# Hybrid decoder layer on one core: memory keys and values computed first, kept in DRAM, and x loaded from GpSimd's queue

## The chip, the cores and the metric

The kernel runs on one core of a Trainium2 chip. A core has five engines that run beside each other: TensorE (PE; its weight loads are shown as PEld), VectorE (DVE), ScalarE (ACT), GpSimd (POOL) and SyncE (SP), which here issues the DMAs. The metric is the device time of one execution in microseconds (us); lower is better. Before the change the median of 3 runs is 2018.0 us (2016.56 to 2018.23).

## What is computed

The reference is one layer of a decoder for a prompt of 1024 tokens and 8 single sample tokens, 1032 rows of width 1024 in all, in float32. Cut to what matters here:

```python
z = x @ w_in                                   # all branches and gates from one projection
xr, yr, q, k, v, xq, g = split(z)
a_out = rg_lru(conv4(xr)) * gelu(yr)           # branch A: a recurrence over the tokens
s_out = sliding_window_attention(q, k, v)      # branch B
mkv = mem_prompt @ w_mem_kv                    # 256 memory tokens -> keys mk, values mv (outputs too)
c_out = mem_attn(xq, mk, mv)                   # branch C: 4 heads of width 256
merged = sum(sigmoid(g_n + b_n) * (branch_n @ w_branch_n))
h = LN(alpha*x + merged @ w_out)
h = LN(alpha*h + SwiGLU(h))
```

The sample tokens use cached keys and values instead of `mk` and `mv`; their window buffers, moved on by one row, are outputs as well.

## The kernel before

Every float32 product is made of three faster ones. `split` (L69) makes a rounded high part on ScalarE and the low part, the difference, on VectorE; `mm3` (L100) then does high x high, high x low and low x high. So each operand of TensorE needs one ScalarE and one VectorE instruction first, and these are listed under L71 and L72 whatever they serve.

The input projection (`project`, L256) goes over 30 units of 256 output columns (`UNITS`, L37). Each is done by a scheme of seven products of quarter matrices (Strassen's, in Winograd's form) instead of eight, so it needs seven combinations of quarters of x. `combos` (L157) makes them, for each half p of the columns of the quarters: four loads (`x_quarter`, L149: 512 features by 258 tokens, 516 KB, issued on SP), four sums or differences, and seven splits into the tiles `th` and `tl` of the pool `tp`, where they stay until the projection ends. The x quarters and the combinations lie in a ring of nine tiles named `z`, which later holds the units' results (`za`, `zb`). The unit's weights come in four loads (`ur`, via `half_raw`, L80: a ring of six raw tiles of 512 columns); `fast_quarter` (L190) makes seven operands `u_0` to `u_6` of them; `fast_product` (L204, lines 212 to 214) does the matmuls into `ub`, `uc` and `ud`. Side jobs, the recurrence (`lru`, L633) and the memory attention of the sample tokens (`dec_mem`, L709), are stepped on by `pump` after every product.

After the projection comes `mem_attention` (L433). `load_mem` (L331) loads and splits the memory tokens. `mem_kv` (L341) computes for one head its two key tiles (`mk`, 24 matmuls each, weights from `wmk`) and its values (`mv`, 48 matmuls, weights from `wmv`), stores them as outputs through a single buffer `kvraw`, and splits them again for use. Each of the four calls stands between the steps of attention: `mem_queries` and `mem_scores` (L386), `mem_values` (L411), and `fill`, which puts in products of branch A's projection (`branch`, L568; `bra`), whose activations `load_branch` (L116) loads as `baL`. Their tiles (`slots0`) lie where `tp` lay. Windowed attention, `out_proj` and `ffn` follow and aren't touched.

The order in which instructions stand on an engine isn't that of the source: a scheduler sorts each engine's list by its own estimates when the kernel is built, within the dependencies. An engine then goes through its list in that order, waits included. `tc.issue_after(x)` asks the scheduler to place what is issued within it after x. A pool's ring of `bufs` tiles makes an instruction that writes a tile wait for the readers of the tile that it reuses.

Of the kernel before, what the change touches and what calls it, by code (L numbers as in the profile page):

```python
# [10 lines left out]
F32 = mybir.dt.float32  # L11
F32R = mybir.dt.float32r
AF = mybir.ActivationFunctionType
ALU = mybir.AluOpType
# [19 lines left out]
HT = T // 2  # L34
QN = T // 4
QS = 272
UNITS = (  # L37
# [16 lines left out]
class Builder:  # L54
# [94 lines left out]
    def x_quarter(self, kh, th, p):  # L149

        t = self.zt(f"x{kh}{th}{p}")
        t0 = HT * th + QN * p
        self.x_loaded = self.nc.sync.dma_start(t.rearrange("p (k n) -> p k n", k=4),
                                               self.io["xT"][:, 4 * kh:4 * kh + 4, t0:t0 + QN]).ins
        return t

    def combos(self, p, quarter):  # L157

        nc = self.nc
        b11, b21, b12, b22 = quarter(0, 0, p), quarter(1, 0, p), quarter(0, 1, p), quarter(1, 1, p)  # L160
        out = []

        def keep(src, i):
            hi, lo = (self.tp.tile([P, 4, QS], F32R, tag="t", name=f"t{e}{i}_{p}", bufs=28) for e in "hl")
            self.split(hi[:, :, :QN], lo[:, :, :QN], src.rearrange("p (k n) -> p k n", k=4))
            out.append((hi, lo))

        keep(b11, 0)
        t1 = self.zt(f"t1_{p}")
        nc.vector.tensor_sub(t1, b11, b12)  # L170
        keep(t1, 1)
        t2 = self.zt(f"t2_{p}")
        nc.vector.scalar_tensor_tensor(t2, t1, -1.0, b22, op0=ALU.mult, op1=ALU.subtract)
        keep(t2, 2)
        keep(b21, 3)
        t3 = self.zt(f"t3_{p}")
        nc.vector.tensor_sub(t3, b22, b12)
        keep(t3, 4)
        keep(b22, 5)
        t4 = self.zt(f"t4_{p}")  # L180
        nc.vector.scalar_tensor_tensor(t4, t2, -1.0, b21, op0=ALU.mult, op1=ALU.subtract)
        keep(t4, 6)
        return out

# [70 lines left out]

    def project(self):  # L256

        nc, io, tc = self.nc, self.io, self.tc
# [6 lines left out]
        n = len(UNITS)  # L265
# [42 lines left out]
    def v_rows(self, zs):  # L308

        nc, io = self.nc, self.io  # L310
        for blk in range(9):
# [7 lines left out]
            if blk == 7:  # L319
                vraw = self.sm.tile([P, 256], F32, tag="kvraw", name="pwv", bufs=1)  # L320
                nc.scalar.copy(vraw, ps)
                nc.sync.dma_start(io["o_pwv"], vraw)
# [7 lines left out]

    def load_mem(self):  # L331
        nc, io = self.nc, self.io
        self.memx = []
        for k in range(KT):
            hi, lo = (self.ph.tile([P, NM], F32R, tag="mem", name=f"mem{e}{k}", bufs=16) for e in "hl")
            if k % 2 == 0:
                raw = self.half_raw(io["memT"][:, k * NM:(k + 2) * NM], 2 * NM, f"mem{k}")
            self.split(hi, lo, raw[:, (k % 2) * NM:(k % 2 + 1) * NM])
            self.memx.append((hi, lo))

    def mem_kv(self, h):  # L341

        nc, io = self.nc, self.io
        mk, mv = [], []
        for m in (2 * h, 2 * h + 1):
            w = self.weights(io["wmk"][m], D, f"wmk{m}")
            ps = self.bank("mm", f"mk{m}")[:, :NM]
            self.mm3(ps, [(w[k], self.memx[k]) for k in range(KT)])
            raw = self.sm.tile([P, 256], F32, tag="kvraw", name=f"mkr{m}", bufs=1)
            nc.scalar.copy(raw, ps)  # L350
            nc.sync.dma_start(io["o_pmk"][:, m, :], raw)
            hi, lo = (self.ph.tile([P, NM], F32R, tag="mk", name=f"mk{e}{m}", bufs=6) for e in "hl")
            self.split(hi, lo, raw)
            mk.append((hi, lo))
        pv = [self.bank("mm", f"mv{h}_{tt}")[:, :256] for tt in range(2)]
        for j in range(4):
            raw = self.half_raw(io["wmv"][2 * h + j // 2][:, (j % 2) * 512:(j % 2 + 1) * 512], 512, f"wmv{h}_{j}r")
            wh, wl = self.half_pair(f"wmv{h}_{j}")
            self.last_split = self.split(wh, wl, raw)
            for tt in range(2):  # L360
                for i in range(2):
                    xh, xl = (a[:, tt * P:(tt + 1) * P] for a in self.memx[2 * j + i])
                    vh, vl = (a[:, i * 256:(i + 1) * 256] for a in (wh, wl))
                    nc.tensor.matmul(pv[tt], xh, vh, start=j + i == 0, stop=False)
                    nc.tensor.matmul(pv[tt], xh, vl, start=False, stop=False)
                    self.last_mm = nc.tensor.matmul(pv[tt], xl, vh, start=False, stop=j + i == 4).ins
        for tt, ps in enumerate(pv):
            raw = self.sm.tile([P, 256], F32, tag="kvraw", name=f"mvr{h}_{tt}", bufs=1)
            nc.scalar.copy(raw, ps)
            nc.sync.dma_start(io["o_pmv"][:, tt, h * 256:(h + 1) * 256], raw)  # L370
            hi, lo = (self.ph.tile([P, 256], F32R, tag="mv", name=f"mv{e}{h}_{tt}", bufs=8) for e in "hl")
            self.split(hi, lo, raw)
            mv.append((hi, lo))
        return mk, mv

# [257 lines left out]
    def lru(self, m, xr, yr):  # L633
# [3 lines left out]
        stt = nc.vector.scalar_tensor_tensor  # L637
        wr = self.z.tile([P, 256], F32, tag="wlr", name=f"wlr{m}", bufs=1)
# [12 lines left out]
        nc.gpsimd.tensor_copy(self.scvo[:, m, 2, :], xr[:, TP:T])  # L651
        wgh, wgl = (self.z.tile([P, 256], F32R, tag=f"wg{e}", name=f"wg{e}{m}", bufs=1) for e in "hl")
        self.split(wgh, wgl, wr)
        a, ti = self.zt(f"tr{m}"), self.zt(f"ti{m}")
        for c, (t0, n) in enumerate(THIRDS):
            xch, xcl = (self.z.tile([P, n], F32R, tag=f"xc{e}", name=f"xc{e}{m}_{c}", bufs=1) for e in "hl")
            self.split(xch, xcl, xc[:, t0:t0 + n])
# [110 lines left out]
    def dec_win_scores(self):  # L768
# [7 lines left out]
        for name, cache, row in (("o_swk", "cwk", krow), ("o_swv", "cwv", self.vd)):  # L776
            nc.sync.dma_start(io[name][:, 0:P - 1, :], io[cache][:, 1:P, :])
            nc.sync.dma_start(io[name][:, P - 1, :], row)
# [281 lines left out]
    def build(self):  # L1060
# [3 lines left out]
        shapes = {"c": [P, KT, T], "s": [P, KT, T], "a": [P, KT, T], "g": [P, 24, T], "xq": [P, KT, 2, TP],  # L1064
                  "q": [P, KT, 2, TP], "k": [P, 2, 2, TP], "v": [P, 8, 512]}
        self.scr = {b: self.dram.tile(n, F32, name=f"scr_{b}") for b, n in shapes.items()}
# [3 lines left out]
        self.ctx.enter_context(pool("edge", "right")).tile([P, 8], F32, name="edge")  # L1070
        with pool("tp", "right") as self.tp, pool("w1") as self.w1, pool("z") as self.z, pool("dp1") as self.dp:
            self.project()
        self.act, self.merged = {}, [[None] * 3 for _ in range(KT)]
# [26 lines left out]
class Finish:  # L1100
# [42 lines left out]
_INS = {  # L1143
    "xT": (P, KT, T), "memT": (P, KT * NM), "wmk": (KT, P, D), "wmv": (8, P, D), "win": (60, P, D),
    "wbr": (24, P, D), "wout": (KT, P, D), "wgu": (2 * NF, P, D), "wdn": (KT, P, NF * P), "wlru": (KT, P, 256),
# [10 lines left out]
def _pack(i):  # L1156
# [15 lines left out]
    x = np.concatenate([f["x_prompt"].reshape(TP, D), f["x_sample"].reshape(NB, D)], axis=0)  # L1172
    o["xT"] = x.T.reshape(KT, P, T).transpose(1, 0, 2)
    o["memT"] = f["mem_prompt"].reshape(NM, D).T.reshape(KT, P, NM).transpose(1, 0, 2).reshape(P, KT * NM)
    wkv = f["w_mem_kv"][0]
# [67 lines left out]
```

## Time and profile before

| | |
|---|---|
| median of 3 runs | 2018.0 us |
| profiled execution | 2021.07 us, of which the span of the trace is 2018.5 |
| granted clock of TensorE, mean | 0.993 |
| VectorE, ScalarE busy | 59%, 44% of the span |
| DMA queues | 235.42 MB, mean 117 GB/s; SP's queue alone 233.17 MB |
| instructions | 35388 |

The profile comes from one execution. A window row shows how long each engine was busy in a stretch. A timeline row has the start, the duration, the engine, the line of the kernel, the operation and its tiles (result <- sources); in brackets stands how long the engine was idle before it and what released it. A wait row sums such idle time: us in total, times, the longest. `L71 ACT ... th` is the high part of a combination of x, `L72 DVE ... tl` its low part.

### The profile page before, as it was taken

Reading aid. Unit: us, or ns where it says so; the run is one execution under the profiler, and the core shown is the slowest. Engines: PE = TensorE matmul, PEld = TensorE weight load, DVE = VectorE, ACT = ScalarE, POOL = GpSimd, SP = SyncE. Lnnn points to the kernel's source line nnn. Section 1 sums busy time; section 2 is a strip of 40 time slices with the busy share of each in tenths; the row PEclk is TensorE's granted clock in tenths of the full one; section 3 lists DMA queues with packets and bytes.
Section 4 is the critical chain, followed back from the end, with each engine's and each line's share of the span. In section 5 each row is a group of like instructions: output and inputs, shape, how many; then the busy total and the mean of one; then the engine's idle time right before and its main releaser. Section 6 shows DMA issues by size and latency. Waiting matters only on the chain.

```text
span 2018.5 us, 35388 instructions
## 1 busy us (share of the span) xinstructions
PE 1960.8 (97%) x13732; PEld 1928.1 (96%) x13732; DVE 1198.8 (59%) x2569; ACT 878.8 (44%) x1922; POOL 112.7 (6%) x160
## 2 busy tenths in 40 slices
PE   6999999999999899999999999999999999999997
PEld 5999999999999898988999999999999999999996
DVE  8797789777766555399776559523222332233457
ACT  5456555646655455298673344322111221122324
POOL 1000010100000000022110003100000000000001
PEclk9999999999999999999999999999999999999998
DMA  5555544462233777567425241111211111111102
GB/s 196 186 170 176 184 155 163 150 225 103 95 132 122 248 226 225 158 168 208 136 85 171 88 136 29 42 42 49 57 42 43 48 54 45 55 42 43 57 29 84
DMA packets 143513, 235.42 MB, mean 117 GB/s; under 512 B 17281, under 2 KB 73681, under 8 KB 143313
## 3 DMA queue, kind: packets, MB, share of 16 engines
q1 hardware_dynamic: 143344, 233.17, 36.5%
q8 instruction: 107, 1.75, 0.4%
q14 instruction: 62, 0.50, 0.1%
HBM read 179.95 MB, written 55.23 MB: 117 GB/s over the span
## 4 chain that ended last, share of the span: by engine, by line
PE 85%; DVE 5%; DMA 5%; ACT 3%; issue 1%; SPq 0%; ACTq 0%; DVEq 0%; POOL 0%; POOLq 0%
PE ub L213 5%; PE ub L214 5%; PE ub L212 5%; PE fg L105 4%; PE fg L106 4%; PE fg L107 4%; PE fu L107 4%; PE fu L105 4%; PE fu L106 4%; PE d L105 3%; PE d L107 3%; PE d L106 3%; PE ud L214 2%; PE ud L213 2%; PE ud L212 2%; PE brs L105 2%
## 5 line engine op out<-in xcount | busy, mean ns | idle before, releaser
L105 PE MATMUL fg<-hH,wfg_h 128*128 128x384 f32 (+1 forms) x528 | 168.3, 319 | 2.9 <-DVE acc L978 1.7
L106 PE MATMUL fg<-hL,wfg_h 128*128 128x384 f32 (+1 forms) x528 | 167.7, 318 | 0.4 <-DVE hL L989 0.4
L107 PE MATMUL fu<-hH,wfu_l 128*128 128x384 f32 (+1 forms) x528 | 167.7, 318 | 0.0
L106 PE MATMUL fu<-hL,wfu_h 128*128 128x384 f32 (+1 forms) x528 | 167.6, 317 | 0.0
L105 PE MATMUL fu<-hH,wfu_h 128*128 128x384 f32 (+1 forms) x528 | 167.5, 318 | 0.0
L107 PE MATMUL fg<-hH,wfg_l 128*128 128x384 f32 (+1 forms) x528 | 167.5, 317 | 0.0
L1007 DVE TENSOR_TENSOR ft<-ft,fu 128x384 f32<-128x384 f32 (+1 forms) x66 | 33.8, 513 | 139.2 <-PE fu L107 139.1
L105 PE MATMUL d<-gH,wd_h 128*128 128x384 f32 (+1 forms) x360 | 114.4, 318 | 0.0
L1005 DVE SCALAR_TENSOR_TENSOR ft<-ft,fg 128x384 f32<-128x384 f32 (+1 forms) x66 | 33.8, 512 | 135.4 <-ACT ft L1004 133.3
L106 PE MATMUL d<-gL,wd_h 128*128 128x384 f32 (+1 forms) x360 | 114.2, 317 | 0.0
L107 PE MATMUL d<-gH,wd_l 128*128 128x384 f32 (+1 forms) x360 | 114.2, 317 | 0.0
L71 ACT CAST gH<-ft 128x384 fp32r<-128x384 f32 (+1 forms) x66 | 31.7, 480 | 174.8 <-DVE ft L1007 174.7
L105 PEld LDWEIGHTS fg<-hH,wfg_h 128*128 128x128 f32 x528 | 99.1, 188 | 3.9 <-DVE acc L978 2.0
L106 PEld LDWEIGHTS fg<-hL,wfg_h 128*128 128x128 f32 x528 | 99.2, 188 | 1.0 <-DVE hL L989 0.9
L107 PEld LDWEIGHTS fg<-hH,wfg_l 128*128 128x128 f32 x528 | 99.3, 188 | 0.0
L107 PEld LDWEIGHTS fu<-hH,wfu_l 128*128 128x128 f32 x528 | 99.2, 188 | 0.0
L105 PEld LDWEIGHTS fu<-hH,wfu_h 128*128 128x128 f32 x528 | 99.2, 188 | 0.0
L106 PEld LDWEIGHTS fu<-hL,wfu_h 128*128 128x128 f32 x528 | 99.2, 188 | 0.0
L1027 DVE SCALAR_TENSOR_TENSOR acc<-d,acc 128x384 f32<-128x384 f32 (+1 forms) x48 | 24.8, 516 | 108.4 <-PE d L107 108.4
L1004 ACT ACTIVATE ft<-fg 128x384 f32<-128x384 f32 (+1 forms) x66 | 30.1, 456 | 135.2 <-PE fg L107 135.2
L212 PE MATMUL ub<-th,u_0h 128*128 128x258 f32 x240 | 69.4, 289 | 15.5 <-ACT th L71 13.5
L212 PE MATMUL ud<-th,u_1h 128*128 128x258 f32 x240 | 69.4, 289 | 2.1 <-ACT th L71 1.4
(953 smaller groups left out, 6854.4 us busy)
## 6 DMA issues: line engine op xcount, KB each, us to landing
ur<-win SPq DMA_DIRECT2D x120, 256.0 KB, 2.7
dck<-cmk SPq DMA_DIRECT2D x32, 256.0 KB, 3.8
dcv<-cmvT SPq DMA_DIRECT2D x32, 256.0 KB, 3.9
st<-scr_q SPq DMA_DIRECT2D x32, 256.0 KB, 5.3
scr_g<-za SPq DMA_DIRECT2D x12, 516.0 KB, 4.1
scr_g<-zb SPq DMA_DIRECT2D x12, 516.0 KB, 5.1
x<-xT SPq DMA_DIRECT2D x8, 516.0 KB, 7.3
scr_a<-ge SPq DMA_DIRECT2D x8, 516.0 KB, 3.2
```

The lines of the kernel that those rows point to most:

```text
L71: ins = self.nc.scalar.copy(hi, src).ins
L105: nc.tensor.matmul(ps, sh, mh, start=i == 0, stop=False)
L106: nc.tensor.matmul(ps, sh, ml, start=False, stop=False)
L107: self.last_mm = nc.tensor.matmul(ps, sl, mh, start=False, stop=closes and i == last).ins
L212: mm(sh[:, w], xh, start=opens and k == 0, stop=False)
L213: mm(sh[:, w], xl, start=False, stop=False)
L214: self.last_mm = mm(sl[:, w], xh, start=False, stop=k == 3).ins
L1004: nc.scalar.activation(t, pg, AF.Tanh, scale=0.5)
L1005: nc.vector.scalar_tensor_tensor(t, t, 1.0, pg, op0=ALU.add, op1=ALU.mult)
L1007: nc.vector.tensor_mul(t, t, pu)
L1027: nc.vector.scalar_tensor_tensor(a, ps, 0.5, a, op0=ALU.mult, op1=ALU.add)
```

## The change

Four things are done, and a few that they need.

- `mem_kv` is done once, for all four heads, as the first thing in `project`, ahead of the first unit's loads: 8 key tiles, then the values of 4 heads. Its pool `mx` is closed before the pools `lr` (new, for the recurrence's small tiles) and `dp1` are opened.
- `combos` has become a generator. It is stepped once after each key tile and after every second value step of `mem_kv`, first for half 0, then for half 1. The order of the combinations and their signs differ a little; the number of VectorE and ScalarE instructions is the same.
- Keys and values go, besides to the outputs, to DRAM (`scr["mk"]`, `scr["mv"]`), and `mem_pair` loads and splits them for one head when `mem_attention` needs them. `mem_attention` has no `mem_kv` and no `load_mem` any more; after the six products at its start it calls `fill(1)` in every second step.
- The x quarters are loaded from GpSimd's queue, out of a copy `xQ` of x in which each partition's row of a quarter lies in one piece. The copy is made by the host's packing.
- `kvraw` has two buffers, `QS` is 264 instead of 272, the `tp` tiles are laid out from combination 6 down to 0, constants are asked for after the first unit's last load, and the copies of the window buffers after the last matmul before them.

```diff
     def x_quarter(self, kh, th, p):
         t = self.zt(f"x{kh}{th}{p}")
-        t0 = HT * th + QN * p
-        self.x_loaded = self.nc.sync.dma_start(t.rearrange("p (k n) -> p k n", k=4),
-                                               self.io["xT"][:, 4 * kh:4 * kh + 4, t0:t0 + QN]).ins
+        self.nc.gpsimd.dma_start(t, self.io["xQ"][kh, 2 * th + p])
         return t
...
+        b11 = self.x_quarter(0, 0, p)
+        keep(0, b11)
+        yield
+        b21 = self.x_quarter(1, 0, p)
+        keep(3, b21)
+        yield
+        b12 = self.x_quarter(0, 1, p)
+        t1 = both(ALU.subtract, "t1", b11, b12)
+        keep(1, t1)
+        yield
+        b22 = self.x_quarter(1, 1, p)
+        t3 = both(ALU.subtract, "t3", b22, b12)
+        yield
+        t2n = both(ALU.add, "t2n", t3, b11)
+        keep(2, t2n, -1.0)
+        yield
+        keep(4, t3)
+        yield
+        keep(5, b22)
+        yield
+        t4 = both(ALU.subtract, "t4", t2n, b21)
+        keep(6, t4)
...
     def project(self, ctx, pool):
+        ts = [[None] * 7, [None] * 7]
+        for i in reversed(range(7)):
+            for p in range(2):
+                ts[p][i] = tuple(self.tp.tile([P, 4, QS], F32R, tag="t", name=f"t{e}{i}_{p}", bufs=28) for e in "hl")
+        with pool("mx") as self.ph:
+            self.mem_kv(chain(self.combos(ts, 0), self.combos(ts, 1)))
         load(0)
-        ts = [self.combos(p, self.x_quarter) for p in range(2)]
-        with tc.issue_after(self.x_loaded):
+        self.lr = ctx.enter_context(pool("lr"))
+        self.dp = ctx.enter_context(pool("dp1"))
+        with tc.issue_after(self.last_load):
             self.load_consts()
             self.load_lru()
...
+        for m in range(KT):
             w = self.weights(io["wmk"][m], D, f"wmk{m}")
             ps = self.bank("mm", f"mk{m}")[:, :NM]
+            self.mm3(ps, [(w[k], memx[k]) for k in range(KT)])
+            put(ps, io["o_pmk"][:, m, :], "mk", m)
+            step()
+        for h in range(4):
...
+                if j % 2:
+                    step()
+            for tt, ps in enumerate(pv):
+                put(ps, io["o_pmv"][:, tt, h * 256:(h + 1) * 256], "mv", 2 * h + tt)
+        for _ in beside:
+            pass
+
+    def mem_pair(self, name, h):
+        hi, lo = (self.ph.tile([P, 2, 256], F32R, tag=name, name=f"{name}{e}{h}", bufs=4) for e in "hl")
+        self.nc.sync.dma_start(lo.bitcast(F32), self.scr[name][:, 2 * h:2 * h + 2, :])
+        self.split(hi, lo, lo.bitcast(F32))
+        return [(hi[:, i, :], lo[:, i, :]) for i in range(2)]
...
     def mem_attention(self, fill):
-        self.load_mem()
-        kv = [None] * 4
         fill(6)
-        kv[0] = self.mem_kv(0)
         last = None
         for n in range(8):
             h, half = n // 2, n % 2
-            ps = self.mem_scores(h, half, self.mem_queries(h, half), kv[h][0])
-            if half == 0 or h == 3:
+            if half == 0:
+                kv = self.mem_pair("mk", h), self.mem_pair("mv", h)
+            ps = self.mem_scores(h, half, self.mem_queries(h, half), kv[0])
+            if half:
                 fill(1)
-            else:
-                kv[h + 1] = self.mem_kv(h + 1)
             if last:
                 self.mem_values(*last)
-            last = h, half, ps, kv[h][1]
+            last = h, half, ps, kv[1]
```

More of the change, by code (lines that the diff above doesn't have):

```diff
@@ L151, in x_quarter, with combos @@
         t = self.zt(f"x{kh}{th}{p}")
-        t0 = HT * th + QN * p
-        self.x_loaded = self.nc.sync.dma_start(t.rearrange("p (k n) -> p k n", k=4),
-                                               self.io["xT"][:, 4 * kh:4 * kh + 4, t0:t0 + QN]).ins
+        self.nc.gpsimd.dma_start(t, self.io["xQ"][kh, 2 * th + p])
         return t
-    def combos(self, p, quarter):
+    def combos(self, ts, p):
         nc = self.nc
[L160 to L183, printed above, removed]
@@ new lines, in keep, with both @@
+        def keep(i, src, sign=1.0):
+            hi, lo = (a[:, :, :QN] for a in ts[p][i])
+            src = src.rearrange("p (k n) -> p k n", k=4)
+            if sign < 0:
+                self.split_scaled(hi, lo, src, sign)
+            else:
+                self.split(hi, lo, src)
+        def both(op, name, a, b):
+            t = self.zt(f"{name}_{p}")
+            nc.vector.tensor_tensor(t, a, b, op)
+            return t
+        b11 = self.x_quarter(0, 0, p)
+        keep(0, b11)
+        yield
@@ L338, in load_mem, with put @@
             self.split(hi, lo, raw[:, (k % 2) * NM:(k % 2 + 1) * NM])
[L339 to L345, printed above, removed]
+            memx.append((hi, lo))
+        def put(ps, out, name, m):
+            raw = self.sm.tile([P, 256], F32, tag="kvraw", name=f"{name}r{m}", bufs=2)
+            nc.scalar.copy(raw, ps)
+            nc.sync.dma_start(out, raw)
+            nc.sync.dma_start(self.scr[name][:, m, :], raw)
@@ L354, in mem_kv @@
[L354 to L366, printed above, removed]
@@ L651, in lru @@
         nc.gpsimd.tensor_copy(self.scvo[:, m, 2, :], xr[:, TP:T])
[L652 removed]
+        wgh, wgl = (self.lr.tile([P, 256], F32R, tag=f"wg{e}", name=f"wg{e}{m}", bufs=1) for e in "hl")
         self.split(wgh, wgl, wr)
```

53 lines of the change are left out of this document (27 added, 26 removed).

## The prediction

> **What bounds the kernel now.** I read the busy table of the page first, then the windows of the run from front to back, then TensorE's own waits, and last the timeline at the two places where those waits stand.
>
> ```profile
> span 2018.5 us, 35388 instructions
> PE 1960.8 (97%) x13732; PEld 1928.1 (96%) x13732; DVE 1198.8 (59%) x2569; ACT 878.8 (44%) x1922; POOL 112.7 (6%) x160
> ```
> ```profile
> 0.00:20.00 20.00, 7.35 (x29) 6.46 (x30) 13.34 (x18) 8.89 (x13) 0.19 (x4) 1.00 0.89 288
> 20.00:40.00 20.00, 14.37 (x88) 13.42 (x87) 17.20 (x18) 12.28 (x18) 6.65 (x8) 0.83 0.58 199
> 40.00:60.00 20.00, 18.28 (x152) 18.03 (x152) 17.03 (x53) 9.68 (x22) 0.00 (x0) 1.00 0.43 154
> ...
> 0.00:100.00 100.00, 78.24 (x559) 75.22 (x560) 76.90 (x161) 48.55 (x86) 7.15 (x14) 0.95 0.58 193
> 100.00:649.00 549.00, 544.68 (x4493) 542.68 (x4492) 428.28 (x848) 314.78 (x593) 32.74 (x38) 1.00 0.45 151
> 649.00:862.00 213.00, 203.75 (x1445) 195.40 (x1445) 104.22 (x236) 99.71 (x252) 2.32 (x13) 0.98 0.67 212
> ```
> ```profile
> PE ub L212 <- ACT th L71: 14.0, 3, 10.0
> PE bra L105 <- ACT baH L71: 6.0, 1, 6.0
> ```
>
> TensorE is busy for 97% of the span, so only the places where it stands count. In a window row the columns are stretch, length, then busy time and number of instructions of PE, weight load, DVE, ACT and POOL, then granted clock, DMA share and GB/s. TensorE loses 21.8 of the first 100 us and 9.3 of the 213 in which memory attention lies; between them only 4.3 of 549. The waits name both: 14.0 us until ScalarE delivers the first `th` (x rounded for TensorE), and 6.0 us until the first `baH`, where branch projection takes over from the input projection. The change touches both.
>
> Busy time hides a second loss: the array runs slowly after a pause. The same 258-column matmul starts every 0.21 us in the rows of 28.75 and 28.96, and every 0.12 us in those of 35.08 and 35.20.
>
> ```profile
> 28.75 0.42 PE L213 MATMUL ub<-tl,u_0h 128*128 128x258 f32 x1
> 28.96 0.42 PE L214 MATMUL ub<-th,u_0l 128*128 128x258 f32 x1
> ...
> 35.08 0.28 PE L214 MATMUL ud<-th,u_1l 128*128 128x258 f32 x1
> 35.20 0.28 PE L212 MATMUL ud<-th,u_1h 128*128 128x258 f32 x1
> ```
>
> So I count loss by work: 29 + 88 + 152 = 269 matmuls in the first 60 us are worth 269 x 0.1195 = 32.1 us at full pace (a few records may be missing). **The start of before costs 60 - 32.1 = 27.9 us.** This is the pot that the change can win from.
>
> **The change, part by part.**
>
> *Memory keys and values first.* The 8 key tiles of 24 matmuls and 4 value groups of 48, 384 matmuls of 256 columns, leave the stretch after 649 us and stand ahead of the first `ub`.
>
> ```profile
> 700.12 0.28 PE L105 MATMUL mk<-memh,wmk_h 128*128 128x256 f32 x1
> ...
> 705.77 0.28 PE L364 MATMUL mv<-wmv_0h,memh 128*128 128x256 f32 x1
> ```
>
> 48 of them take 5.65 us, so 384 are worth 45.2 us. That work is only moved. The change wins if TensorE finishes it by 27.9 + 45.2 = 73.1 us, and loses by as much as it is later. What decides this is when the operands come, and there I go by the order of the built instructions on each engine. TensorE takes memory tile 0, then tiles 1 to 7, then the values, then `ub`. VectorE does ten small splits (eight of mem, two of `wmk0`) interleaved with the first x quarters, **then all the rest of both halves of x, and only then the first split of `wmk1`**. ScalarE has the same order. So "beside" holds for one key tile of eight: TensorE can do 24 matmuls and then stands behind the whole of x, since each engine starts its instructions in the built order, as the rows of before do.
>
> VectorE ahead of `wmk1` has 22 instructions of 1032 columns (14 low parts, 8 combinations), 2 of 512 and 8 of 256. Their steps from start to start:
>
> ```profile
> 20.08 1.23 DVE L181 SCALAR_TENSOR_TENSOR t<-t,x 128x1032 f32<-128x1032 f32 x1
> ...
> 21.22 1.23 DVE L72 TENSOR_TENSOR tl<-t,th 128x1032 fp32r<-128x1032 f32 x1
> ...
> 8.28 0.69 DVE L196 TENSOR_TENSOR us<-us,ur 128x512 f32<-128x512 f32 x1
> 8.88 0.68 DVE L196 TENSOR_TENSOR us<-ur,ur 128x512 f32<-128x512 f32 x1
> ...
> 671.58 0.76 DVE L72 TENSOR_TENSOR meml<-mem,memh 128x256 fp32r<-128x256 f32 x2 [0.34 <-ACT memh L71]
> ```
>
> That is 22 x 1.14 + 2 x 0.60 + 8 x 0.34 = 29.0 us without a gap. It can't begin before the first load has landed and been rounded: in before the first `ur` was used at 3.38, so about 4 us. **The floor for the first split of `wmk1` is 33 us.**
>
> ```profile
> 0.72 1.81 SPq L82 DMA_DIRECT2D ur<-win  x4
> 2.57 2.86 SPq L153 DMA_DIRECT2D x<-xT  x4
> 3.38 0.62 ACT L71 CAST u_0h<-ur 128x512 fp32r<-128x512 f32 x1 [1.39 <-DMA ur<-win]
> ...
> 8.89 1.05 ACT L71 CAST th<-x 128x1032 fp32r<-128x1032 f32 x1
> ...
> 8.00:10.00 2.00, 0.00 (x0) 0.00 (x0) 1.97 (x4) 1.72 (x3) 0.00 (x0) 1.00 1.08 375
> 10.00:12.00 2.00, 1.21 (x4) 0.92 (x5) 2.00 (x4) 1.51 (x3) 0.00 (x0) 1.00 1.09 367
> ```
>
> To the floor I add the gaps of its chains. Six SP loads of 256 KB and the x quarters of 516 KB share engines that were already full at 370 GB/s, so I estimate the first quarter at 6 us and the second at 9, and each must be rounded by ScalarE (1.05) before VectorE's turn: 2.5 + 1.5 us of gap. In the second half the last three quarters wait for buffers: nine `z` tiles, eight used by the first half, the tenth free when `t2n` is done at about 20 us, after which POOL issues three transfers of 516 KB against six SP loads of 256 KB; 3.2 MB at 370 GB/s is 8.5 us, so the last lands at about 29 and VectorE waits another 2. Dependent steps cost another 1. Together 7: **tile 1 starts at about 40 us**, with bounds 33 and 46. TensorE's 24 matmuls of tile 0 are over by about 18, and 22 us of standing follow.
>
> From there 360 matmuls are left: 42.4 us, and 2 for the slow pace after the pause, like 6.5 us at half pace at 28 us. Splits (0.60 on VectorE for 1.41 us of matmuls), six raw buffers and SP's order, with each store of a result ahead of later loads, leave no gap that I can find: the prefetch is ten half tiles deep. DMA isn't the end here: 9.4 MB of weights and memory, 4.2 of x, 4.2 of stores are 51 us at 350 GB/s. TensorE is done at 84.5, bounds 77 and 93; with small seams I take 86. **Start: 86 - 73.1 = +13 us**, bounds +4 and +20.
>
> *x from GpSimd's queue.* The 2.86 us in which SP issued four quarters go from its path, but VectorE is the bound, so nothing is gained. The price of a GpSimd issue isn't in this trace; the nearest rows are SP's 0.7 us for a quarter and POOL's own small copies:
>
> ```profile
> L650 POOL COPY scvo<-scv 128x16 f32<-128x16 f32 x8 | 6.6, 881 | 30.1 <-DMA scv<-scv 30.1
> ```
>
> I take 1 us, near POOL's 0.88; two or three times that moves `x_672` by 2 to 4 us, which the upper bound holds. The Trainium skill, SBUF — State Buffer, section "SBUF: two separate sides", says that descriptors of such transfers are written by GpSimd through a port that VectorE can lock; no run here shows it yet, and by it the loads would come later still. The Trainium skill, DMA: Bandwidth & Descriptors, section "Issuing engines are not separate DMA queues", says that issuing from several engines saves only issue time; the share of 1.08 above agrees.
>
> *What follows the memory work.* The first unit's loads stand between result stores in SP's order, landing about when TensorE needs them: 0 to 2 us, in the seams. Before has one more stall while the first recurrence starts, 10 - 50 x 0.12 = 4.0 us here:
>
> ```profile
> 70.00:75.00 5.00, 3.52 (x23) 2.64 (x21) 4.50 (x10) 2.39 (x6) 0.00 (x0) 1.00 0.00 0
> 75.00:80.00 5.00, 4.72 (x27) 4.67 (x27) 5.00 (x17) 2.55 (x6) 0.00 (x0) 0.66 0.39 126
> ```
>
> The unit and its helpers are the same, so I leave it unchanged, bounds -4 and +2.
>
> *The takeover and memory attention.*
>
> ```profile
> 669.50:675.50 6.00, 0.03 (x1) 0.03 (x1) 2.42 (x12) 2.29 (x6) 0.00 (x0) 0.78 0.97 336
> 675.50:700.00 24.50, 24.50 (x144) 24.20 (x144) 17.10 (x38) 13.37 (x32) 0.00 (x0) 0.92 0.90 302
> 700.00:862.00 162.00, 158.74 (x1133) 150.91 (x1132) 77.57 (x174) 75.34 (x198) 2.12 (x12) 1.00 0.67 206
> ...
> 670.02 0.33 SPq L1124 DMA_DIRECT2D scr_g<-zb  x1
> 670.40 3.89 SPq L122 DMA_DIRECT2D baL<-scr_a  x7
> ```
>
> The stop of 6 us is the `baL` loads, issued only after the last gate was stored at 670.02. In the new order the first stands ahead of that store and the other seven behind it, and mem's two splits no longer stand ahead of `baH` on ScalarE: -1, bounds -6 and +1. The 162 us behind it lose the 45.2 and, in the same measure, 11.5 MB of transfers; keys and values come back as 2.1 MB of loads with the same sums of splits. Its 3.3 us of idle time may go, or grow as there is less work to cover score and softmax: -1, bounds -3 and +4. Later pool openings, the second store buffer, the smaller `QS` and the moved window copies lie beside TensorE's work: 0.
>
> Sum: +13 - 1 - 1 = **+11 us**. Profiled: 2021.07 (span 2018.5 and 2.6 around it) becomes 2032. The median of the runs, 2018.0, is 3.1 below the profiled one; with the same +11 it becomes **2029 us**.
>
> **The rivals.** *GpSimd's loads are late.* If each costs several us, the first half gets gaps too and tile 1 starts at 46: 93 - 73 = +20, less 2: 2036. For it: three loads wait for buffers and POOL does them in order. Against it: the first five need nothing and the engine is idle.
>
> *The middle pays for the start* (the other side). The place is the takeover: if all of its 6.0 us, the 3.3 behind it and the 4.0 at 70 to 80 go, 13.3 come back; with tile 1 near the floor (+4 to +6) the kernel gets faster by about 8: 2010. It decides once tile 1 starts before 40 with all given back, or before 36 with the takeover and one more. For it: seven buffers less pressure on DMA (0.97 busy there). Against it: seven of the eight loads still follow the last gate's store.
>
> *It does what it says*: half of the splits run beside x, tile 1 to 7 interleaved, TensorE done near 73. Time 2018 less 2: 2016. The built order speaks against it.
>
> *The middle gets worse.* Queries, keys, values and gates squeeze 4 MB into each 17 us of TensorE's work (240 GB/s against 206): +6 on the forecast, 2035.
>
> **How the numbers follow.** Forecast 0.58, late loads 0.17, worse middle 0.08: together 0.83, nearly all slower. Middle pays 0.09 and does what it says 0.08 share the rest. Within 0.2% (4 us, about what a measurement of this kernel can tell from no change) lie the second of these and the lowest tail of the forecast, 0.03. Slower 0.80, same 0.11, faster 0.09. The range reaches from 2016, the interleaved case, to 2039, the upper bound of the start with no gain in the middle.
>
> **What would show it.** Right: TensorE does 24 matmuls of `mk` by 18 us, then stands until about 40 waiting for a `wmk` split, VectorE full of `tl` and combinations meanwhile; the first `ub` at 86 or so; a takeover of about 5 us. Wrong if tile 1 starts before 33 (then the order isn't what VectorE keeps), if VectorE itself stands over 10 us waiting for x (late loads), or if the takeover's stop is gone.

## The result and the profile after

The changed kernel takes 2036.5 us (median of 6 runs, 2033.4 to 2038.9) against 2017.9 for the kernel before (6 runs): ratio 1.0091, 95% interval 1.0078 to 1.0104. It is slower by 18.5 us. Its profiled execution took 2036.36 us, with a span of 2034.1: 15.3 us over the profiled execution of before, 15.6 by span.

First the busy table of the page, then the windows that answer to those of before (columns as there). The matmul work is the same to within 4 us; in the first 100 us TensorE is busy 17.7 us less than in before.

```profile
span 2034.1 us, 35455 instructions
PE 1964.7 (97%) x13732; PEld 1931.2 (95%) x13732; DVE 1198.7 (59%) x2561; ACT 877.4 (43%) x1914; POOL 116.3 (6%) x168
```
```profile
0.00:20.00 20.00, 5.94 (x22) 5.05 (x22) 8.36 (x16) 8.23 (x14) 3.06 (x9) 1.00 0.71 263
20.00:40.00 20.00, 1.10 (x4) 0.51 (x3) 18.74 (x18) 9.80 (x11) 1.60 (x3) 1.00 0.49 171
40.00:60.00 20.00, 16.88 (x115) 16.59 (x116) 11.69 (x16) 10.64 (x20) 0.00 (x0) 1.00 0.55 180
60.00:80.00 20.00, 18.16 (x135) 17.39 (x134) 6.40 (x10) 6.93 (x14) 0.00 (x0) 0.91 0.67 218
...
0.00:100.00 100.00, 60.59 (x424) 57.62 (x425) 55.52 (x82) 45.77 (x80) 8.09 (x20) 0.98 0.65 219
```

From 20 to 40 us VectorE is full (18.74 of 20) and TensorE starts two matmuls, the last of tile 0 (a window row also counts those that began before its stretch and end in it). The waits of TensorE from 40 to 100 us and the timeline around the stop name what ends it: the high and low parts of `wmk1`, which stand on ScalarE and VectorE right behind the last part of x.

```profile
PE mk L105 <- ACT wmk_h L71: 20.1, 1, 20.1
PE mv L383 <- ACT wmv_3h L71: 1.3, 1, 1.3
```
```profile
40.31 1.05 ACT L71 CAST th<-t 128x1032 fp32r<-128x1032 f32 x1
41.26 0.61 ACT L71 CAST wmk_h<-wmk1r__225 128x512 fp32r<-128x512 f32 x1
```
```profile
42.03 1.23 DVE L72 TENSOR_TENSOR tl<-t,th 128x1032 fp32r<-128x1032 f32 x1
43.17 0.68 DVE L72 TENSOR_TENSOR wmk_l<-wmk1r__225,wmk_h 128x512 fp32r<-128x512 f32 x1
```

SP's issues hold a second piece. Its seventh issue is a 1 MB copy of a window cache (`o_swk`, from DRAM to DRAM), then the store of tile 0's result, and only then `wmk1`. In the kernel before the same two copies are issued at 15.7 and 27.0 us, behind the first unit's loads. The change asks for the copies only after the last matmul before them, yet the first is issued at 3.62 us, and no matmul of this run starts before 13.6: a mark on TensorE's list did not hold them back on SP's.

```profile
3.06 0.53 SPq L82 DMA_DIRECT2D wmk0r__186<-wmk  x1
3.62 0.90 SPq L799 DMA_DIRECT2D o_swk<-cwk  x1
22.25 0.35 SPq L364 DMA_DIRECT2D o_pmk<-mkr  x1
22.64 0.43 SPq L365 DMA_DIRECT2D scr_mk<-mkr  x1
23.20 0.37 SPq L82 DMA_DIRECT2D wmk1r__225<-wmk  x1
```

Where the time went can be read from four marks, each the first matmul of its kind in the view of one tile: `ub` (projection), `ub` of the last unit, `bra` (branch projection) and `bs` (window attention). For kernels that do the memory work late, 45.2 us are added to the first three marks, so that all count the same work; before's first `ub` is set at full pace, 27.9 + 45.2 = 73.1, as in the prediction.

| | first `ub` | last unit | first `bra` | first `bs` | span |
|---|---|---|---|---|---|
| before | 73.1 | 696.9 | 720.7 | 851.0 | 2018.5 |
| after | 93.3 | 713.9 | 735.0 | 864.6 | 2034.1 |
| difference | +20.2 | +17.0 | +14.3 | +13.6 | +15.6 |

The start loses 20; 3.2 come back by the last unit, 2.7 at the takeover, 0.7 in memory attention; 2.0 are lost again behind it. (The stretches on the two sides of the first `bs` don't hold the same work in the two kernels; the last part says what that changes.)

### The profile page after: what moved, and what is told of

The parts are those of the page before. It is cut to its first block, busy times and chain, and to the rows that moved or that the text cites. A ratio compares the mean times of both kernels' runs of the same rounds, so it can differ in the third digit from the quotient of the medians.

```text
span 2034.1 us, 35455 instructions
## 1 busy us (share of the span) xinstructions
PE 1964.7 (97%) x13732; PEld 1931.2 (95%) x13732; DVE 1198.7 (59%) x2561; ACT 877.4 (43%) x1914; POOL 116.3 (6%) x168
## 4 chain that ended last, share of the span: by engine, by line
PE 87%; DVE 5%; DMA 4%; ACT 3%; issue 1%; SPq 0%; ACTq 0%; DVEq 0%
PE ub L225 5%; PE ub L223 5%; PE ub L224 5%; PE fg L105 4%; PE fg L106 4%; PE fg L107 4%; PE fu L107 4%; PE fu L105 4%; PE fu L106 4%; PE d L105 3%; PE d L107 3%; PE d L106 3%; PE ud L225 3%; PE ud L224 3%; PE ud L223 3%; PE brs L105 1%
## 5 line engine op out<-in xcount | busy, mean ns | idle before, releaser
L1049 DVE SCALAR_TENSOR_TENSOR acc<-d,acc 128x384 f32<-128x384 f32 (+1 forms) x48 | 24.8, 516 | 108.4 <-PE d L107 108.4
L521 ACT ACTIVATE bp<-bp,bst 128x257 f32<-128x257 f32 (+1 forms) x128 | 62.7, 492 | 18.8 <-DVE bst L517 18.6
```

The lines of the kernel that those rows point to most:

```text
L521: nc.scalar.activation(x, x, AF.Exp, bias=st[:, g:g + 1], scale=-1.0, accum_out=st[:, 4 + g:5 + g])
L1049: nc.vector.scalar_tensor_tensor(a, ps, 0.5, a, op0=ALU.mult, op1=ALU.add)
```

## The experiments

The theories. **Order**: TensorE lost its 20 us because all of x stood ahead of `wmk1`'s splits. **Copies**: the transfers of the two window copies delayed x and the loads. **Queue**: x through GpSimd comes too late. From the second set on there is **planner**: a copy costs the loads that the scheduler's order puts behind it, wherever it stands. Ratios are to executions of the kernel before that were run with each set (medians 2018.2 to 2020.2), with 95% intervals; the marks of all runs stand in one table at the end of this section.

### Where the copies stand, and where x stands

*Copies late* (one word of the changed kernel; the copies are then issued at 696.5 and 729.3 us):

```diff
-            with self.tc.issue_after(self.last_mm):
+            with self.tc.issue_after(self.last_load):
                 nc.sync.dma_start(io[name][:, 0:P - 1, :], io[cache][:, 1:P, :])
```

> The two 1 MB copies of the window caches are issued behind the last load of the projection instead of at 3.6 and 56.2 us; nothing else is edited, and in the built order that alone puts wmk1's loads ahead of tile 0's store and interleaves wmk1's to wmk7's splits with the combinations of x. Order theory (TensorE lost its 20 us because all of x stood ahead of wmk1's splits): tile 1 starts by 22 us, the first ub by 77, 16 us earlier than in the changed kernel (93.3), time about 2020 (2016 to 2024). Copies theory (the transfers themselves delayed x and the loads): about the same here, 2020; it is told apart by the next run. Queue theory (x through GpSimd comes too late): x still comes from there, so VectorE stands over 8 us for x and the time stays over 2030.

Measured: 2024.0 us, ratio 1.0016 (1.0004 to 1.0028). With a load of SP's own as the mark the copies stay behind it. With no other edit the built order is interleaved, as "beside" promises, and TensorE has no long stop: 156 matmuls from 20 to 40 us. The first `ub` comes at 67.1, 10 us better than expected and 6.0 better than in before. ScalarE's waits for x come to 5.4 us in all, for the first two quarters, so the queue theory falls here. But the lead is gone by the first `bs`, which is 0.6 behind before.

```profile
20.00:40.00 20.00, 18.90 (x156) 18.49 (x156) 16.67 (x22) 12.59 (x23) 1.60 (x3) 1.00 0.96 316
```

*Copies late, x first*: the same with `wmk1`'s splits held behind x (`x_hi` and `x_lo` are the last high and low part of a combination).

```diff
         for m in range(KT):
+            if m == 1:
+                for _ in beside:
+                    pass
+            with ExitStack() as behind:
+                if m == 1:
+                    behind.enter_context(self.tc.issue_after(self.x_hi))
+                    behind.enter_context(self.tc.issue_after(self.x_lo))
+                w = self.weights(io["wmk"][m], D, f"wmk{m}")
```

> As the run before, copies late and wmk1's loads early, but both halves of x are held ahead of wmk1's splits on ScalarE and VectorE, as in the changed kernel. Order theory: the stand stays; the first x lands about 2.5 us earlier and nothing else is gained ahead of tile 1, which starts at 37 to 39 instead of 41.6; behind it the 4 us lost at 66 to 77 go; first ub at about 86, time 2029 (2026 to 2032). Copies theory: without the transfers TensorE gets its operands, first ub by 78, time as in the run with the copies late alone, within 3 us, about 2020.

Measured: 2044.5 us, ratio 1.0119 (1.0095 to 1.0143); 20.5 over the run before by the medians. The stop is back (20.1 us), the first `ub` at 88.1. The order theory has its sign and size at the start; the end was missed by 15 us, 11 of them between `bra` and `bs` (140.9 us against 129.6 in the changed kernel), where the run before lost its lead as well (139.5).

*Interleaved*: the copies stay in front, each step of the combinations is held behind the splits of its key or value tile (`last_split` and `key_lo` are their last high and low part).

```diff
-        step = lambda: next(beside, None)
+        def step():
+            with self.tc.issue_after(self.last_split), self.tc.issue_after(self.key_lo):
+                next(beside, None)
```

> The copies stay at the front as in the changed kernel, but each step of the combinations is held behind the splits of its key or value tile on ScalarE and VectorE. The order of SP's queue has tile 0's store still ahead of wmk1's loads. Order theory: the splits of wmk1 go as soon as it has landed; its loads leave SP after tile 0's result (about 19 to 22 us) and land some 4 us later, so tile 1 starts at 25 to 28 and the first ub comes about 14 us earlier than 93.3, at 79 to 81; time 2022 (2019 to 2026). Copies theory: the transfers are where they were, so the time stays at 2033 to 2037.

Measured: 2022.6 us, ratio 1.0016 (1.0005 to 1.0027), as the order theory had it, with a copy of 1 MB at 3.8 us as in the changed kernel. First `ub` at 81.2, 12.1 earlier than there. That the transfer delays x is out: the first x is used at 8.80 us with the copy in front and at 8.99 without it (the run with the copies at the end). But the copies in front aren't free here. The first `ub` comes 14.1 us later than with the copies late, since SP issues `wmk1` behind tile 0's store, at 20.86 us instead of 11.61, and tile 1 starts at 24.4.

```profile
8.80 1.05 ACT L71 CAST th<-x 128x1032 fp32r<-128x1032 f32 x1 [4.41 <-DMA x<-xQ]
```
```profile
8.99 1.05 ACT L71 CAST th<-x 128x1032 fp32r<-128x1032 f32 x1 [4.38 <-DMA x<-xQ]
```

*Four result buffers*: memory results in four tiles instead of two, in a pool of their own phase (the other user of the old ring goes back to one tile); else the changed kernel.

```diff
-            raw = self.sm.tile([P, 256], F32, tag="kvraw", name=f"{name}r{m}", bufs=2)
+            raw = self.ph.tile([P, 256], F32, tag="kvraw", name=f"{name}r{m}", bufs=4)
```

> As the changed kernel, but four buffers for the memory results instead of two, so that ScalarE doesn't wait 5.4 us for a store before it takes the next result (order on VectorE ahead of tile 1 as in the changed kernel). If the two buffers cost the 4 us that TensorE loses at 68 to 77: first ub at 89 to 90, time 2033 (2031 to 2034). If the 1 MB copy issued at 56.2 is what holds up the stores and the value loads behind it, more buffers do nothing: 2036 within 1.5. The stand up to 41 us stays by every theory.

Measured: 2037.6 us, ratio 1.0081 (1.0057 to 1.0105): nothing gained. SP's issues in this run show that the buffers weren't it. The value weights `wmv_1` stand in the built order behind the stores of key results, and SP waits there for one result after the other; TensorE waits 4.2 us for `wmv_1`. The 1 MB copy among them holds SP for 1.0 us of waiting, the results for 5.7.

```profile
55.02 0.38 SPq L82 DMA_DIRECT2D wmv_0r<-wmv  x1
55.45 0.73 SPq L799 DMA_DIRECT2D o_swv<-cwv  x1
56.28 0.38 SPq L364 DMA_DIRECT2D o_pmk<-mkr  x1
...
67.04 0.42 SPq L365 DMA_DIRECT2D scr_mk<-mkr  x1
67.55 0.40 SPq L82 DMA_DIRECT2D wmv_1r<-wmv  x1
```

### What a copy costs where

If only the copies' place spoiled the run with the copies late, a place with idle DMA engines should win.

*Copies in the middle*: behind the loads of unit 10.

```diff
             st[u] = self.fast_load(u, io["win"][a], io["win"][b])
+            if u == 10:
+                self.mid_load = self.last_load
...
-            with self.tc.issue_after(self.last_mm):
+            with self.tc.issue_after(self.mid_load):
```

> As the run with the copies late, but the two copies are issued behind the loads of unit 10, near 270 us, where TensorE has work and the DMA engines are half idle. The order of the memory phase is the same as there (interleaved, wmk1's loads ahead of tile 0's store). If the late copies cost that run its lead (at the first matmul of branch projection it was 8.6 us ahead of the kernel before, at the first score of window attention 0.6 behind): first ub at 67, first bra at 712, first bs at 841 to 843, time 2010 (2007 to 2014), faster than both kernels. If the stretch of memory attention loses those 9 us for another reason (its different order): 2020 to 2024 again.

Measured: 2034.2 us, ratio 1.0073 (1.0058 to 1.0089). The expectation failed by 24 us: the first `ub` was as early as expected (69.1), but now the projection stopped, behind each copy (257.5 and 318.9 us). The windows of the second stop, SP's waits and TensorE's there:

```profile
340.00:350.00 10.00, 10.00 (x84) 10.00 (x83) 3.19 (x6) 3.11 (x7) 0.00 (x0) 1.00 0.00 1
350.00:360.00 10.00, 7.21 (x59) 6.92 (x57) 3.70 (x9) 3.17 (x8) 0.00 (x0) 1.00 0.01 2
```
```profile
SPq L743 <- DVE dcj L747: 24.8, 1, 24.8
```
```profile
PE ub L223 <- ACT u_0h L71: 9.4, 1, 9.4
```
```profile
334.79 0.33 SPq L1148 DMA_DIRECT2D scr_g<-zb  x1
360.04 0.38 SPq L743 DMA_DIRECT2D dck<-cmk  x1
360.48 1.88 SPq L82 DMA_DIRECT2D ur<-win  x4
```

This is the mechanism in the open. For 20 us the DMA engines move 1 and 2 GB/s: nothing is short of bandwidth. SP stands 24.8 us at one load (`dck`) whose buffer VectorE hasn't freed yet, and the next unit's four loads stand behind it in the order that the scheduler built with the copy ahead of them. TensorE runs out and waits 9.4 us. So the price of this copy isn't its transfer but the order that stands behind it. With the copies at the end (below) SP puts loads of `ur` between the eight `dck` loads of the same head, and TensorE waits 0.9 us in all from 200 to 420. The first stop shows on another list: TensorE waits 7.4 us for a result `zb` of VectorE, which had itself stood 8.7 us at an instruction of the recurrence.

*Middle, x first*: the same hold as above on top of this.

> As the run with the copies in the middle, with all of x held ahead of wmk1's splits. This gives the price of the order alone, with no copy near the front or in memory attention. Order theory: tile 1 at 41, first ub at 88, first bs near 862, time 2031 (2028 to 2034), 20 us over the run before. If the order is worth only what the copies added to it: within 5 us of the run before.

Measured: 2056.6 us, ratio 1.0185 (1.0168 to 1.0202): 22.3 over the run before (20 expected); the level was missed for the reason just told.

*Before, copies in the middle*: the same edit in the kernel before.

> The kernel before, with its two copies (issued at 15.7 and 27.0 us there) put behind the loads of unit 10 and nothing else changed by hand. If they are hidden there behind the combinations of x, on VectorE 1.23 us each: 2018 (2015 to 2020). If they take bandwidth from the second half of x, which VectorE waits for: up to 6 us faster, 2012; then part of the lead of the run with the copies in the middle is not due to the memory work at all.

Measured: 2040.8 us, ratio 1.0103 (1.0086 to 1.0119). Neither bound holds: the start gained (602 matmuls in the first 100 us against 559), and then SP stood 24.8 us for the same `dck` load, and TensorE waited the same 7.4 and 9.4 us. The old kernel has the same weakness; it has nothing to do with the memory work.

*Middle, x from SP*: one word, `self.nc.sync` for `self.nc.gpsimd` in `x_quarter`.

> As the run with the copies in the middle, but the quarters of x are issued by SP, between wmk's halves and the stores in the built order, instead of by GpSimd. If the queue as such costs nothing, as forecast: time within 4 us of that run. If GpSimd's issue is slow or late: 5 to 10 us faster, since the first quarter can land at 6 instead of 8.9. Queueing behind the stores can also make it slower, by the wait of the fourth quarter for two results, 2 to 4 us, if VectorE then stands.

Measured: 2039.1 us, ratio 1.0096 (1.0080 to 1.0111), 4.8 over the run with x from GpSimd. The first key matmul goes from 13.5 to 8.4 us, the first `ub` from 69.1 to 69.7: what the first tile gains is waited for later.

### Copies where nothing stands behind them

*Copies at the end*: traced after the feed-forward part. The copies are issued at 1910.4 and 1963.8 us, and by the built lists the order of all engines is that of a kernel without them (no such kernel was run).

```diff
-            with self.tc.issue_after(self.last_mm):
-                nc.sync.dma_start(io[name][:, 0:P - 1, :], io[cache][:, 1:P, :])
...
                         self.ffn(self.out_proj(self.merged))
+                        with tc.issue_after(self.last_load):
+                            for name, cache in (("o_swk", "cwk"), ("o_swv", "cwv")):
+                                nc.sync.dma_start(io[name][:, 0:P - 1, :], io[cache][:, 1:P, :])
```

> The two copies stand behind the last weight load of the kernel, near 1937 us, where SP has nothing else to issue until 1986; the built order of every engine is then the same as that of a kernel without the copies. Planner theory (a copy costs the time of the loads that the built order puts behind it, wherever it stands): first ub at 67 and first bra at 712 as with the copies late, then the 129 us from first bra to first bs of the changed kernel, so first bs at 841.5; end 2011 (2007 to 2015), faster than both kernels by 0.3% or more. If the copies themselves are slow (and not the order around them), the outputs queued behind them in SP's queue at 1986 end later: over 2016.

Measured: 2009.8 us, ratio 0.9960 (0.9947 to 0.9974), faster than both kernels. The windows of its start:

```profile
0.00:20.00 20.00, 6.15 (x28) 5.13 (x28) 8.51 (x17) 9.23 (x17) 3.05 (x9) 1.00 0.76 266
20.00:40.00 20.00, 18.80 (x153) 18.19 (x153) 16.89 (x22) 13.48 (x24) 1.59 (x3) 1.00 0.96 323
40.00:60.00 20.00, 19.11 (x156) 18.32 (x155) 19.82 (x25) 15.81 (x27) 0.00 (x0) 1.00 0.90 280
```

*Before, copies at the end*: the same edit in the kernel before.

> The kernel before with the same edit. In the run of before with the copies in the middle TensorE had done 602 matmuls in its first 100 us against 559, worth 43 x 0.12 = 5 us; that gain stays here and the loss of some 25 behind 240 us goes. Planner theory: 2013 (2010 to 2016). Then the memory work first, on equal terms, is worth 2 us, not 20. If the copies at 15.7 and 27.0 were hidden behind x: 2018 (2016 to 2020), and memory first is worth 7.

Measured: 2012.9 us, ratio 0.9971 (0.9960 to 0.9983), as the planner theory said. So of the lead of the run above, some 6 us are the copies' and only 3.0 the memory work's; the two intervals overlap, so that these 3 aren't certain.

*End, x first*:

> As the changed kernel with the copies at the end, all of x held ahead of wmk1's splits on ScalarE and VectorE; behind row 109 of VectorE the built order is the same. Order theory: first ub at 87 to 88, time 20 us over that kernel's, 2031 (2028 to 2034). If the order alone costs little: within 5 us of it.

Measured: 2031.6 us, ratio 1.0060 (1.0046 to 1.0074), 21.8 over the copies at the end. SP issues `wmk1` at 11.11 here, not at 23.20, and still its split waits: the order on VectorE and ScalarE is enough for the whole stop.

```profile
11.11 0.33 SPq L82 DMA_DIRECT2D wmk1r__281<-wmk  x1
```
```profile
20.00:40.00 20.00, 0.79 (x2) 0.50 (x2) 18.74 (x18) 10.14 (x12) 1.59 (x3) 1.00 0.33 109
```

*End, x from SP*:

> As the changed kernel with the copies at the end, with the quarters of x issued by SP instead of GpSimd. With the copies in the middle that edit moved the first key matmul from 13.5 to 8.4 us, but the first ub from 69.1 to 69.7 and the time by +4.8. Queue costs nothing: first ub within 2 us of 67, time 2010 (2007 to 2015), that is within 0.25% of the kernel with x from GpSimd. Queue late: the earlier first tile is kept up to the first ub, 62, and the time is 2005. If queueing behind stores costs (the 4.8 of the pair before is real): 2014.

Measured: 2011.9 us, ratio 0.9963 (0.9950 to 0.9976): the same as with GpSimd's queue; the 4.8 us of the pair in the middle don't come back. The queue costs and gains nothing that these runs can tell. The Trainium skill, DMA: Bandwidth & Descriptors, section "Issuing engines are not separate DMA queues", had it so; these two times agree with it.

### The marks of all runs

| | first `ub` | last unit | first `bra` | first `bs` | span | time |
|---|---|---|---|---|---|---|
| copies late | 67.1 | 689.0 | 712.1 | 851.6 | 2022.0 | 2024.0 |
| late, x first | 88.1 | 709.3 | 732.2 | 873.1 | 2043.5 | 2044.5 |
| interleaved | 81.2 | 702.1 | 723.5 | 852.0 | 2021.8 | 2022.6 |
| four buffers | 95.3 | 715.7 | 737.0 | 865.7 | 2036.1 | 2037.6 |
| middle | 69.1 | 711.8 | 733.3 | 861.6 | 2032.1 | 2034.2 |
| middle, x first | 87.0 | 731.7 | 752.9 | 880.5 | 2052.1 | 2056.6 |
| before, middle | - | 716.8 | 740.0 | 874.3 | 2041.4 | 2040.8 |
| middle, x from SP | 69.7 | 715.4 | 736.6 | 866.4 | 2036.8 | 2039.1 |
| end | 66.2 | 686.4 | 707.6 | 837.7 | 2008.0 | 2009.8 |
| before, end | - | 688.9 | 712.6 | 843.1 | 2010.6 | 2012.9 |
| end, x first | 86.6 | 705.9 | 727.1 | 857.0 | 2028.2 | 2031.6 |
| end, x from SP | 69.6 | 689.9 | 711.5 | 840.2 | 2009.5 | 2011.9 |

(Before's two rows have the 45.2 us added in the second and third column, as above.)

From before to after by span: the copies off their old place -7.9 (2018.5 to 2010.6), memory first with x interleaved -2.6 (to 2008.0), x ahead of `wmk1` +20.2 (to 2028.2), and the early copies with the stores ahead of the loads +5.9 (to 2034.1): +15.6 in all. These are single executions, and spans of the kernel before alone go from 2014.2 to 2024.8; by the ratios of medians the four steps are -5.9, -2.2, +20.2 and +6.3. The sizes also hold for this sequence only. Taken the other way, the early copies cost 13.8 with x interleaved (2008.0 to 2021.8) and x first then 12.3 (to 2034.1): with the copies in front the loads of `wmk1` are late already, and the two delays overlap.

## Why the prediction was right, and where it was off

*All the rest of x, then `wmk1`.* Right. Tile 0 ended at 21.8 (forecast 18), tile 1 began on ScalarE at 41.3 and on VectorE at 43.2 (forecast 40, bounds 33 and 46), and three pairs of runs price that order at 20.5, 22.3 and 21.8 us. In these pairs the copies are out of the front; in the fourth, with the copies in front, it costs 12.3 by span.

*The start, +13.* It was +20.2, at the upper bound of +20. Tile 1 came 1.9 us later than forecast (41.9 against 40), and more was lost behind it. The step that failed is that six raw buffers and SP's order leave no gap behind tile 1, beside 2 us of slow pace and "small seams". From 40 to 80 us TensorE starts 247 matmuls, worth 29.1 us at 45.2 / 384 = 0.1177, in the 38.1 from the start of tile 1: 9.0 lost where some 3.5 had been counted. The pace was slow to 50:

```profile
42.00:44.00 2.00, 0.81 (x3) 0.52 (x3) 2.00 (x4) 1.96 (x4) 0.00 (x0) 1.00 0.00 0
44.00:46.00 2.00, 2.00 (x9) 2.00 (x10) 1.66 (x3) 0.00 (x0) 0.00 (x0) 1.00 0.56 169
46.00:48.00 2.00, 2.00 (x11) 2.00 (x11) 0.69 (x1) 0.62 (x1) 0.00 (x0) 1.00 0.86 284
48.00:50.00 2.00, 2.00 (x11) 2.00 (x11) 0.69 (x1) 0.89 (x2) 0.00 (x0) 1.00 0.56 203
50.00:52.00 2.00, 2.00 (x19) 2.00 (x18) 0.69 (x1) 0.62 (x1) 0.00 (x0) 1.00 0.54 146
...
72.00:74.00 2.00, 0.86 (x4) 0.66 (x5) 0.69 (x1) 0.62 (x1) 0.00 (x0) 0.97 0.99 308
74.00:76.00 2.00, 2.00 (x12) 2.00 (x11) 0.69 (x1) 1.34 (x3) 0.00 (x0) 0.50 0.38 142
```

Rows side by side count a matmul that crosses their border twice; 29 matmuls start in those 8 us. They are worth 3.4, so 4.6 are lost there: a wait of 1.2 for the low part of `wmk1`, and then one start every 0.21 us instead of 0.12, at a granted clock of 1.00 in the rows. From 68 to 78, 49 start, worth 5.8 us in 10: 4.2 lost, where the value weights were late (1.8 of waiting, the rest slow starts around it, with a clock of 0.50 in the row of 74). They stood in SP's queue behind stores that waited for results; the four-buffer run, in which that order stays, loses as much. That is the gap that I had not found, though the order of SP was there to be read.

The prediction's own counts have the border matmuls twice as well: 265 start in the first 60 us of before, not 269, and 46 from 70 to 80, not 50. So the start of before costs 28.3 us instead of 27.9, its stall at 70 to 80 4.5 instead of 4.0, and the loss at the start is 19.8 rather than 20.2. No reading changes by it.

*The moved window copies: 0.* Right as a transfer, wrong as a cause. Their place, not the memory work, decided the order that the prediction took as given: with that one word changed, the same kernel is built interleaved and takes 2024.0. I had priced them beside TensorE's work and had not asked what the scheduler puts behind them. That it holds a copy for much longer than the chip does fits all runs (the DMA engines stand idle behind it in the middle); its estimates are in no trace, so this reason for the order is argued, not shown. Nor was the mark of `issue_after` tried apart from a copy.

*x from GpSimd's queue: 0.* Right (2009.8 and 2011.9). Forecast landings of 6 and 9 us for the first two quarters were 2 to 3 us too early: first uses at 8.80 and 10.75, with the DMA engines full (shares of 1.03 to 1.11 from 6 to 14 us). An issue took 0.57 us (five in 2.87), not 1. The port lock of the Trainium skill (SBUF — State Buffer, "SBUF: two separate sides"), which the prediction named, left no sign: the three late issues took 0.53 to 0.54 us while VectorE went from one 1.23 us instruction to the next. That section of the Trainium skill ties the lock to certain kinds of VectorE instruction, those in a two-port mode above all. No run here shows that these were of such a kind, so the rule itself stays untested.

```profile
1.26 2.87 POOL L152 DMA_DIRECT2D x<-xQ  x5 [0.83 <-POOLq L1251]
20.92 0.53 POOL L152 DMA_DIRECT2D x<-xQ  x1 [16.79 <-DVE tl L72]
22.40 0.53 POOL L152 DMA_DIRECT2D x<-xQ  x1 [0.95 <-DVE t L170]
25.06 0.54 POOL L152 DMA_DIRECT2D x<-xQ  x1 [2.13 <-DVE t L170]
```

*The stall at 70 to 80, unchanged.* It is gone. In before TensorE stands there at the recurrence's first matmul (`xch`) and then for `u_1`. In the changed kernel the recurrence's first matmul starts at 147.6 us, and TensorE is busy throughout from 120 to 200. Its one stop, of 1.5 us at 95 to 100, is another: it waits for `u_1` of the first unit, in the seam that the forecast had at 0 to 2 us.

```profile
72.50 0.42 PE L105 MATMUL g<-xch,wgh 128*128 128x344 f32 x1 [0.68 <-ACT xch L71]
```
```profile
PE ud L223 <- ACT u_1h L71: 0.9, 1, 0.9
PE ud L225 <- DVE u_1l L72: 0.6, 1, 0.6
```
```profile
120.00:150.00 30.00, 30.00 (x249) 29.92 (x248) 23.16 (x64) 11.85 (x25) 0.92 (x2) 1.00 0.57 184
150.00:200.00 50.00, 50.00 (x414) 49.95 (x413) 38.65 (x84) 30.73 (x56) 2.19 (x3) 1.00 0.50 167
```

With 25 starts in those 5 us some 2.0 are lost, against 4.5 in before; the 2.5 between them are most of the 3.2 that come back by the last unit.

*Takeover -1, memory attention -1, later parts 0.* By the marks -2.7, -0.7 and +2.0. The wait for `baH` is 3.9 us instead of 6.0.

```profile
PE bra L105 <- ACT baH L71: 3.9, 2, 3.2
```

The other two are not on equal work. The changed kernel has eleven steps of `fill` ahead of windowed attention where before has twelve, and 376 matmuls of `bra` start before its first `bs` against 393; all other matmuls before that mark are the same in number. The 17 have 384 columns and start every 0.174 us (median), so they are worth 3.0. On equal work memory attention costs +2.3 (inside its bounds of -3 and +4, on the other side of the forecast), and the later parts -1.0. The same shift is in every run that does the memory work first.

*The sum.* The forecast of +11 was right in sign and in its main cause. The time came 7.5 us above the 2029: the start cost 7.2 more than forecast, and the rest gave back 2.6 more by span. Without that the time would have stood at 2039, the end of the range.

*The rivals.* Late loads (2036): the time is there, the mechanism is not, since tile 1 came at 41 to 43 and VectorE had no long wait for x. The middle pays: it gave back 6.6 us by the marks and 3.6 on equal work, not the 13.3 that it needed. "It does what it says" (2016) is the kernel that the copies prevented: with them out of the way it takes 2009.8. "The middle gets worse" (2035): on equal work memory attention did, but by 2.3 us, with the takeover 2.7 better; which wait makes the 2.3 isn't followed here.

## What to carry to other kernels

Where a scheduler orders the engines' lists, a transfer that nobody waits for can be the dearest line of a change: look at what stands behind it in the queue, not at its bytes, and try it at a place with nothing behind it. Read the list of SP as well as that of VectorE, and look there for stores that wait for results ahead of loads. Give both kernels the same treatment before a gain is put down to the idea: 6 of the 9 us here were to be had without it.

## What was not expected of the hardware

With the DMA engines full in both, more came in per microsecond with `xQ`: the run with the copies at the end moved 407 GB/s from 6 to 14 us, the kernel before 359. The two DMA views of that stretch differ in the packets: 1172 of 2.8 KB on average against 2467 of 1.2 KB.

```profile
DMA packets 1172, 3.26 MB, mean 407 GB/s; under 512 B 135, under 2 KB 135, under 8 KB 1172
```
```profile
DMA packets 2467, 2.87 MB, mean 359 GB/s; under 512 B 110, under 2 KB 2035, under 8 KB 2467
```

The other loads in that stretch differ too, and no run changes the packing alone, so the packets as the cause are not shown. The first use of x didn't gain by it: 8.99 and 8.80 us with `xQ`, 8.89 without.
